# Hybrid attention/RWKV/conv block on one core: the bias masks inside the recurrence, another order of the stages, 128-row query-key passes and a token-major softmax

## The chip, the cores and the metric

The kernel runs on one core of one Trainium2 chip. Time is device microseconds of that core; lower is better. A run of the kernel before took 1196.58 us (median of three, 1184.8 to 1198.01). The profile shown here is one further execution.

## What is computed

One decoder layer on x of 512 tokens by 1024 channels, in float32, cut to the parts that matter here:

```python
h = rmsnorm(x) * (1 + sc1) + sh1
z_attn, z_rwkv, z_conv, z_gate = split(h @ w_in)
# attention: 8 heads of 64, an indexer picks min(256, s // 4) = 128 keys for each query
score = sum_h(relu(qi_h @ ki.T) * wi_h);  keep the top 128 causal keys
logits = q @ k.T / 8 + rel_bias[t5_bucket(pos_q - pos_k)]      # 32 buckets, 8 heads
o_attn = softmax(logits over the kept keys) @ v
o_rwkv = rwkv7_mix(z_rwkv)         # a recurrence over the tokens, group norm, gate
o_conv = c_b * causal_dwconv(c_c * c_x, sc_conv_w)
gates = sigmoid(z_gate)            # 3 branches of 1024 channels
merged = gates[0]*(o_attn @ w_b[0]) + gates[1]*(o_rwkv @ w_b[1]) + gates[2]*(o_conv @ w_b[2])
x = x + g1 * (merged @ w_o)
x = x + g2 * conv_glu_ffn(rmsnorm(x) * (1 + sc2) + sh2);  final rmsnorm
```

## The kernel before, in words

Every large product is done with both operands split into a high and a low part, so that a block of 128 rows takes three matmuls: lines 177, 178 and 179 in `mm_t` (weights as the stationary operand, 512 tokens moving) and lines 188 to 190 in `mm_n` (V columns, 256 wide). `weights` loads a raw block over the SP queue, ACT copies it to the high part (line 163) and POOL subtracts it for the low part (line 165). Such a triple for one 128x128 block is called a weight triple below. A column of z (`z_col`, 8 triples) ends in one of three PSUM banks named `mm`; everything else on TensorE uses a ring of five banks named `sd`.

A scheduler sets the order on each engine: it takes the program text as the order of importance and pulls work forward whose inputs and buffers are free. Weight triples of later stages thereby stand as filler between the small steps of the serial stages. `tc.high_priority` with a negative offset makes a step less important than its place says; `tc.issue_after` keeps it behind a named instruction.

The stages in the order of time: the norm, columns of z for the RWKV branch; the solve of 31 steps on DVE (lines 569 and 571), whose result goes through DRAM and back (`blk`, `Dm`) and becomes `TT`; the recurrence over 8 chunks of 64 tokens (lines 604 to 645: `Xs`, line 610, from products at 608; `UV`, line 619, from products at 617; the state `S`, lines 636 and 638, from products at 625; each has a fresh `sd` bank); group norm and the output of that branch (lines 669 to 674); the conv columns (lines 693 to 702), pulled forward by the scheduler into the solve and the recurrence; the columns of the attention (`att_cols`), with the bias masks and some `ada` steps between them; the V columns (line 188 on); the indexer (`two_pass`, lines 800 and 801, relu on ACT, weighted sum on DVE, lines 832 and 834) and the top 128 by 16 rounds of MAX8 and MATCH_REPLACE8 for each query block (lines 839 and 840); the attention; three branches with gates, `w_o`, the feed-forward part.

The bias. `posq` holds the key-side positions, `thr` 32 thresholds for each of four key blocks. For a key block b and half of the thresholds, 16 masks (`mk`, line 721, DVE, 0 or 1 in f16) of 128 by up to 512 queries are made; 32 matmuls of 128x32 with `dmat` for each query block (line 727) turn them into the bias of 8 heads; ACT scales them into `stage` (line 733, two instructions for each bank) and a DMA writes them to `bias_d` in DRAM.

The attention. For each of four head pairs and each of four query blocks, POOL adds the top-128 mask to the bias tile `bt` (line 867). `two_pass` makes the logits: the first pass has the key's high part on both halves of the 128 rows against the query's high and low part, the second the key's low part against the query's high part on 64 rows. DVE adds the bias and takes the maximum (line 874), negates it (line 876), ACT takes exp and the sum (line 878), DVE scales the probabilities (line 881), TensorE transposes them (line 885), ACT copies them to `pT` (line 889); after four query blocks, line 894 multiplies `pT` with V and ACT copies the result to `o_at` (line 897). `merged` of the branches lies in a left pool that is opened after the attention's pools are closed; the first write to it follows the gates (line 920).

`ada` are 96 pieces of the conditioning matrix, each a load and one multiply-add on DVE (line 217); they can stand anywhere before the feed-forward part and are handed out in portions, by `next(ada, None)`.

Of the kernel before, what the change touches and what calls it, by code (L numbers as in the profile page):

```python
# [20 lines left out]
H, HD = 8, 64  # L21
# [38 lines left out]
def hybrid_block(ctx, tc, ins, out, consts, dbg=None, stop=99):  # L60
# [286 lines left out]
    def rel_pos(name, shape, aps, pos0, pool, keep=None):  # L347

        pi, lo_i = (T(name + x, shape, I32, pool=pool) for x in "il")
        for dst, ap in aps:  # L350
            SP.dma_start(dst(pi), ap)
        DVE.tensor_scalar(lo_i, pi, 0xFFFF, None, op0=ALU.bitwise_and)
        DVE.tensor_scalar(pi, pi, 16, None, op0=ALU.arith_shift_right)
        rel = T(name, shape, pool=keep or pool)
# [3 lines left out]
        return rel  # L358

    def bias_operands():  # L360
# [7 lines left out]
        thr = rel_pos("thr", [128, 4, 32], [  # L368
            ((lambda t, b=b: t[:, b, :]), dram("positions", b * 128, [[0, 32], [32, 4], [1, 32]])) for b in range(4)], pos0, start.pool, sb)
        DVE.tensor_scalar(thr, thr, kc[:, K_THR:K_THR + 1], None, op0=ALU.add)  # L370
# [25 lines left out]
        return pos0, thr, pw, dmat  # L396

    with tc.issue_after(h_last):
        pos0, thr, pw, dmat = bias_operands()
# [155 lines left out]
    ep.close()  # L555

# [9 lines left out]
    for s_ in range(31):  # L566
# [4 lines left out]
        DVE.tensor_tensor(Ts[:, s_ + 1:, :w], Ts[:, s_ + 1:, :w], t_, op=ALU.add)  # L571
# [28 lines left out]

    S_ = None
    for c in range(8):
        if c:
# [80 lines left out]
    cvp = left_pool("cvp")  # L684
    o_cv = T("o_cv", [128, 4, 512], pool=cvp.pool)

# [6 lines left out]
    for m in range(4):  # L693
        ps_c = z_col(C_CONV + 512 + m * 128)
        cc = wk()
        ACT.activation(cc, ps_c, AF.Copy)
        ps_x = z_col(C_CONV + 1024 + m * 128)
        DVE.tensor_tensor(cc, cc, ps_x, op=ALU.mult)
        cy = wk()
        conv3(cy, cc, cw[:, m, :])  # L700
        ps_b = z_col(C_CONV + m * 128)
        DVE.tensor_tensor(o_cv[:, m, :], cy, ps_b, op=ALU.mult)  # L702
    tap("o_conv", o_cv)


    adp = left_pool("adp")
    bi = right_pool("bi")

    posq = rel_pos("posq", [128, S], [(lambda t: t, dram("positions", 0, [[0, 128], [1, S]]))], pos0, bi.pool)
    bias_d = tc.dram_tile([4, 128, H, 4, 128], F32, name="bias_d")  # L710

    def bias_steps():
        for b in range(4):
            n = S - 128 * b
            stage = {}
            for half in range(2):
# [6 lines left out]
                for qb in range(b, 4):  # L723
# [5 lines left out]
                    if half == 0:  # L729
                        stage[qb] = T("stage", [128, 8, 4, 2, 16], tag="stage", bufs=4, pool=bi.pool)  # L730
# [595 lines left out]
```

## Time and profile before

| | us |
|---|---|
| median of three runs | 1196.58 (1184.8 to 1198.01) |
| the profiled execution | 1197.88 |
| its span, first to last instruction | 1196.2 |
| TensorE busy | 1093.3 (91% of the span) |
| DVE busy | 763.9 (64%) |
| ACT busy | 447.3 (37%) |
| POOL busy | 363.7 (30%) |
| mean granted TensorE clock | 0.95 of full speed |

The profile gives for each engine the time in which it had an instruction under way; on TensorE instructions overlap, so that an instruction's duration is longer than the distance to the next one's start. A window view gives busy time and number of instructions of each engine in a stretch of the span, with the granted clock and what the DMA engines did. A line view groups instructions, with the idle time of the engine ahead of them and what ended it.

### The profile page before, as it was taken

To read this page: it belongs to the slowest core of one execution; us is meant where nothing else is said; L and a number is where in the kernel's file an instruction comes from. 1 tells how busy PE (TensorE), PEld (TensorE's weight loads), DVE (VectorE), ACT (ScalarE), POOL (GpSimd) and SP (SyncE) were. 2 spreads that over 40 slices of the span, in tenths; PEclk is the share of its full clock that TensorE was granted. 3 is DMA by queue.
4 is the path that set the end of the run, shared out by engine and by line. 5 is a ranking of instruction groups with operands and counts; after the bars stand their busy time and mean duration, and the time that the engine had idled before them with its cause. 6 is when DMAs were issued, how large, how long until landed. Compare 5 with 4: busy or idle time off the path is not lost.

```text
span 1196.2 us, 17528 instructions
## 1 busy us (share of the span) xinstructions
PE 1093.3 (91%) x6710; PEld 877.2 (73%) x6710; DVE 763.9 (64%) x1363; ACT 447.3 (37%) x765; POOL 363.7 (30%) x254
## 2 busy tenths in 40 slices
PE   4889899799999989998887999998899999999996
PEld 3667678577767875876655778877898888888885
DVE  5888777732587828798555454468866766762326
ACT  4243332132334322422333443446543444542213
POOL 3233233322222430565455210003443455200001
PEclk9899899899989975998899999999999999999998
DMA  9641123322336990279766343522233333462201
GB/s 324 183 107 42 39 75 91 88 61 60 115 98 193 302 247 9 76 208 233 211 186 152 91 132 101 176 84 89 75 85 106 87 90 106 141 229 92 97 5 71
DMA packets 191074, 148.26 MB, mean 124 GB/s; under 512 B 18148, under 2 KB 167038, under 8 KB 190990
## 3 DMA queue, kind: packets, MB, share of 16 engines
q1 hardware_dynamic: 162605, 122.57, 35.5%
q10 hardware_dynamic: 23056, 14.53, 4.1%
q0 software_dynamic: 5328, 10.03, 3.8%
q8 instruction: 53, 0.87, 0.3%
q14 instruction: 32, 0.25, 0.1%
HBM read 128.48 MB, written 18.63 MB: 123 GB/s over the span
## 4 chain that ended last, share of the span: by engine, by line
PE 59%; DVE 21%; issue 8%; DMA 7%; ACT 3%; POOL 2%; SPq 0%; ACTq 0%; DVEq 0%; POOLq 0%
PE mm L177 6%; PE mm L179 6%; PE mm L178 6%; DMA xraw<-in_ada_w 3%; PE sd L177 2%; PE sd L178 2%; PE sd L179 2%; PE sd L801 2%; PE sd L1250 2%; PE sd L1252 2%; PE sd L1251 2%; PE sd L1047 2%; DVE acc L217 2%; PE sd L1049 2%; PE sd L1048 2%
## 5 line engine op out<-in xcount | busy, mean ns | idle before, releaser
L165 POOL TENSOR_TENSOR wlo<-wraw,whi 128x1024 fp32r<-128x1024 f32 (+1 forms) x70 | 157.1, 2246 | 279.6 <-ACT whi L163 222.1
L178 PE MATMUL mm<-h_lo,whi 128*128 128x512 f32 (+2 forms) x496 | 203.3, 410 | 1.5 <-DVE h_lo L1076 1.5
L177 PE MATMUL mm<-h_hi,whi 128*128 128x512 f32 (+2 forms) x496 | 203.7, 412 | 0.7 <-DVE o_cv L702 0.7
L179 PE MATMUL mm<-h_hi,wlo 128*128 128x512 f32 (+2 forms) x496 | 203.4, 410 | 0.0
L163 ACT ACTIVATE whi<-wraw 128x1024 fp32r<-128x1024 f32 (+1 forms) x86 | 80.2, 935 | 221.2 <-PE mm L178 95.2
L178 PEld LDWEIGHTS mm<-h_lo,whi 128*128 128x128 f32 (+1 forms) x496 | 96.2, 194 | 24.5 <-issue 3.3
L177 PEld LDWEIGHTS mm<-h_hi,whi 128*128 128x128 f32 (+1 forms) x496 | 96.0, 194 | 23.0 <-issue 4.2
L179 PEld LDWEIGHTS mm<-h_hi,wlo 128*128 128x128 f32 (+1 forms) x496 | 96.3, 194 | 22.1 <-issue 2.4
L1017 DVE TENSOR_TENSOR wlo<-wraw,whi 128x1024 fp32r<-128x1024 f32 x46 | 64.5, 1403 | 58.9 <-ACT whi L1016 58.3
L1016 ACT ACTIVATE whi<-wraw 128x1024 fp32r<-128x1024 f32 x46 | 48.7, 1059 | 75.7 <-PE sd L1252 27.7
L217 DVE SCALAR_TENSOR_TENSOR acc<-xraw,ccol,acc 128x512 f32<-128x512 f32 x56 | 55.7, 994 | 26.1 <-DMA xraw<-in_ada_w 25.7
L1034 POOL TENSOR_TENSOR fS<-wraw 128x512 f32<-128x512 f32 x13 | 19.8, 1526 | 155.3 <-DMA wraw<-in_ffn_w_up 142.5
L1047 PE MATMUL sd<-mg_hi,shi 128*128 128x256 f32 x156 | 45.1, 289 | 7.8 <-DVE p L1190 7.8
L1017 DVE TENSOR_TENSOR slo<-wraw,shi 128x1024 fp32r<-128x1024 f32 x28 | 34.9, 1247 | 21.6 <-ACT shi L1016 21.5
L721 DVE TENSOR_SCALAR mk<-posq,thr 128x512 f16<-128x512 f32 (+3 forms) x128 | 44.7, 424 | 4.1 <-PE sd L727 4.1
L1293 POOL TENSOR_TENSOR f<-f 128x512 f32<-128x512 f32 x4 | 5.7, 1415 | 134.8 <-ACT wk L993 134.8
L177 PE MATMUL sd<-h_hi,whi 128*128 128x512 f32 x112 | 44.5, 397 | 0.0
L1048 PE MATMUL sd<-mg_lo,shi 128*128 128x256 f32 x156 | 44.4, 285 | 0.0
L1049 PE MATMUL sd<-mg_hi,slo 128*128 128x256 f32 x156 | 44.4, 285 | 0.0
L178 PE MATMUL sd<-h_lo,whi 128*128 128x512 f32 x112 | 44.3, 396 | 0.0
L179 PE MATMUL sd<-h_hi,wlo 128*128 128x512 f32 x112 | 44.2, 395 | 0.0
L177 PE MATMUL mm<-o,whi 128*128 128x512 f32 x96 | 39.9, 416 | 3.2 <-DVE modc L203 3.2
(521 smaller groups left out, 2780.7 us busy)
## 6 DMA issues: line engine op xcount, KB each, us to landing
wraw<-in_w_in SPq DMA_DIRECT2D x61, 512.0 KB, 4.3
xraw<-in_ada_w SPq DMA_DIRECT2D x96, 256.0 KB, 4.4
wraw<-in_ffn_w_up SPq DMA_DIRECT2D x44, 512.0 KB, 3.9
wraw<-in_ffn_w_down SPq DMA_DIRECT2D x22, 512.0 KB, 3.4
wraw<-in_w_branch SPq DMA_DIRECT2D x24, 256.0 KB, 3.8
bias_d<-stage ACTq DMA_DIRECT2D x10, 512.0 KB, 5.2
wraw<-in_w_o SPq DMA_DIRECT2D x8, 512.0 KB, 3.8
z_att<-wk ACTq DMA_DIRECT2D x12, 256.0 KB, 2.2
```

The source lines that it names most:

```text
L163: ACT.activation(hi, raw, AF.Copy)
L165: lo_engine[0].tensor_tensor(lo, raw, hi, op=ALU.subtract)
L177: PE.matmul(ps, hi[:, k, :], ahi[:, k0 + k, :], start=start and k == 0, stop=False)
L178: PE.matmul(ps, hi[:, k, :], alo[:, k0 + k, :], start=False, stop=False)
L179: PE.matmul(ps, lo[:, k, :], ahi[:, k0 + k, :], start=False, stop=stop and k == kt - 1)
L217: DVE.scalar_tensor_tensor(acc, raw, ck, acc, op0=ALU.mult, op1=ALU.add)
L721: DVE.tensor_scalar(m_[:, :n], posq[:, b * 128:], thr[:, b, gg:gg + 1], None, op0=ALU.is_ge)
L1016: ACT.activation(hi, src, AF.Copy)
L1017: DVE.tensor_tensor(lo, src, hi, op=ALU.subtract)
L1047: PE.matmul(ps, w[0][:, k], b[0][:, k], start=first and k == 0, stop=False, skip_group_check=True)
L1048: PE.matmul(ps, w[0][:, k], b[1][:, k], start=False, stop=False, skip_group_check=True)
L1049: PE.matmul(ps, w[1][:, k], b[0][:, k], start=False, stop=k == 3, skip_group_check=True)
```

## The change

1. The bias masks. `bias_steps` now stands ahead of the recurrence, and one step (16 masks, their matmuls, the ACT evictions and the DMAs) is offered at the head of each chunk and then ahead of each attention column, with a priority 3000 lower than its place. Query blocks are taken in pairs, so a mask is at most 256 wide: 192 masks (128 of 256, 64 of 128) in the place of 128 (32 each of 512, 384, 256, 128). The stage of a bank is one ACT instruction (20) in the place of two (40), and a half goes to DRAM at once: 20 DMAs of 256 KB in runs of 256 bytes in the place of 10 of 512 KB.
2. `thr` is worked out from `posq` after the solve; at the start, the four loads and six DVE instructions for it are gone.
3. The conv columns stand behind the attention in the text.
4. The loads of the indexer's operands (`qi`, `ki`, `wiT`) stand right behind the columns they come from, all on POOL. The pools `att` and `ix` are opened earlier, that of `ada` later; the `ada` steps between the attention columns are gone, and a gate takes three of them in the place of four.
5. `two_pass`: the low part of the key is loaded onto both halves, so the second pass takes 128 rows as the first does (and adds the product of the two low parts). `kl` needs two DMAs in the place of one.
6. The softmax: the DVE step gives the negated maximum at once; exp of a head follows its own maximum; the probabilities are not scaled (line 881 is gone, and 876). `pT` of one head and query block is the stationary operand and V moves (line 873 of the changed kernel: 80 matmuls of 128x64 in the place of 64 of up to 512 columns), the result `o_tok` is scaled by 1/sum on DVE (16 instructions), and 16 transposes bring it back to `o_at`. `o_tok` and two buffers of `kl` and `pT` make the attention's pool about 2 KB per partition larger.

```diff
+    posq = T("posq", [128, S], pool=bi.pool)
+    with tc.issue_after(sub_last):
+        rel_pos(posq, dram("positions", 0, [[0, 128], [1, S]]))
+        thr = T("thr", [128, 4, 32])
...
+    def bias_steps():
+        for b in range(4):
+            for qbs in [q for q in ((0, 1), (2, 3)) if q[1] >= b]:
+                qbs = [q for q in qbs if q >= b]
+                n = 128 * len(qbs)
+                for half in range(2):
+                    mk = []
+                    for g in range(16):
+                        gg = half * 16 + g
+                        m_ = T("mk", [128, 256], F16, tag="mk", bufs=17, pool=bi.pool)
+                        DVE.tensor_scalar(m_[:, :n], posq[:, qbs[0] * 128:qbs[0] * 128 + n], thr[:, b, gg:gg + 1], None, op0=ALU.is_ge)
+                        mk.append(m_)
+                    for i, qb in enumerate(qbs):
+                        ps = sd_bank()
...
+                        stage = T("stage", [128, 8, 64], tag="stage", bufs=2, pool=bi.pool)
+                        ACT.activation(stage, ps.rearrange("p (k h) -> p h k", h=8), AF.Copy, scale=pw[:, 0:1])
+                        ACT.dma_start(bias_d[qb, :, :, b, half * 64:half * 64 + 64], stage)
+                    yield
+    def bias_step():
+        with tc.high_priority(offset=-3000), tc.issue_after(sub_last):
+            next(bias, None)
     S_ = None
     for c in range(8):
+        bias_step()
         if c:
             px = sd_bank()
...
     def att_cols(c0, slot, scale):
         for i in range(4):
-            if slot == 1:
-                next(ada, None)
-            if slot < 2:
-                next(bias, None)
+            bias_step()
             split_out(z_att[slot, i], z_col(c0 + i * 128), scale)
...
     def two_pass(ps, q, hh, q0, k_hi, k_lo, n):
-        r = slice(hh * 64, hh * 64 + 64)
         PE.matmul(ps[:, :n], q[:, hh, q0:q0 + 128], k_hi[:, :n], start=True, stop=False)
-        PE.matmul(ps[:, :n], q[r, hh, q0:q0 + 128], k_lo[r, :n], start=False, stop=True)
+        PE.matmul(ps[:, :n], q[:, hh, q0:q0 + 128], k_lo[:, :n], start=False, stop=True)
...
-        kh, kl = M("kh", [128, 2, 512], F32R), M("kl", [128, 512], F32R)
-        for hh in range(2):
-            POOL.dma_start(kh[hh * 64:(hh + 1) * 64], z_att[1, pr, :, 0, :].rearrange("(h r) t -> r h t", h=2))
-        POOL.dma_start(kl, z_att[1, pr, :, 1, :])
-        pT = M("pT", [128, 4, 640], bufs=1)
+        kh, kl = M("kh", [128, 2, 512], F32R), M("kl", [128, 2, 512], F32R)
+        for i, k in enumerate((kh, kl)):
+            for hh in range(2):
+                POOL.dma_start(k[hh * 64:(hh + 1) * 64], z_att[1, pr, :, i, :].rearrange("(h r) t -> r h t", h=2))
+        o_tok = M("o_tok", [128, 4, 128])
...
-                DVE.tensor_tensor_reduce(lg[hh][:, :n], ps[:, :n], bt[:, hh, :n], 1.0, -3.0e38, op0=ALU.add, op1=ALU.max,
+                DVE.tensor_tensor_reduce(lg[hh][:, :n], ps[:, :n], bt[:, hh, :n], -1.0, 3.0e38, op0=ALU.add, op1=ALU.min,
                                          accum_out=rs[:, 0, hh:hh + 1])
-            DVE.tensor_scalar(rs[:, 1], rs[:, 0], -1.0, None, op0=ALU.mult)
+                ACT.activation(lg[hh][:, :n], lg[hh][:, :n], AF.Exp, bias=rs[:, 0, hh:hh + 1], scale=-1.0,
+                               accum_out=rs[:, 1, hh:hh + 1])
+            DVE.reciprocal(rs[:, 2], rs[:, 1])
+            po = sd_bank()
             for hh in range(2):
-                ACT.activation(lg[hh][:, :n], lg[hh][:, :n], AF.Exp, bias=rs[:, 1, hh:hh + 1], accum_out=rs[:, 2, hh:hh + 1])
-            DVE.reciprocal(rs[:, 0], rs[:, 2])
-            for hh in range(2):
-                DVE.tensor_scalar(lg[hh][:, :n], lg[hh][:, :n], rs[:, 0, hh:hh + 1], None, op0=ALU.mult)
...
+                pT = M("pT", [128, 512])
+                ACT.activation(pT[:, :n], pt[:, :n], AF.Copy)
+                h = 2 * pr + hh
+                for b in range(qb + 1):
+                    PE.matmul(po[:, hh * 64:(hh + 1) * 64], pT[:, b * 128:(b + 1) * 128], vtok[:, b, h * 64:(h + 1) * 64],
+                              start=(b == 0), stop=(b == qb))
+            DVE.tensor_tensor(o_tok[:, qb].rearrange("p (h d) -> p h d", h=2), po[:, :128].rearrange("p (h d) -> p h d", h=2),
+                              rs[:, 2].unsqueeze(2).to_broadcast([128, 2, 64]), op=ALU.mult)
...
+    for m in range(4):
+        ps_c = z_col(C_CONV + 512 + m * 128)
...
     branch(1, split_o(o_rw), True, False)
```

How the instructions stand on the engines. TensorE of the kernel before, from the end of chunk 0 of the recurrence (line 625) to the products of chunk 1 (line 608); `mm<-h_hi,whi` and the like are weight triples:

```order
L625 MATMUL sd<-UV,HYL 128x64 x7
L177 MATMUL mm<-h_hi,whi 128x512
L178 MATMUL mm<-h_lo,whi 128x512
L179 MATMUL mm<-h_hi,wlo 128x512
L608 MATMUL sd<-S,AR 64x64
L177 MATMUL mm<-h_hi,whi 128x512
L608 MATMUL sd<-S,AR 64x64 x7
```

One triple lies between the two steps. TensorE of the changed kernel, where chunk 0 ends (line 663 is the former 625); the triples that begin here are followed by more of their kind:

```order
L663 MATMUL sd<-UV,HYL 128x64
L177 MATMUL mm<-h_hi,whi 128x512
L178 MATMUL mm<-h_lo,whi 128x512
L179 MATMUL mm<-h_hi,wlo 128x512
L177 MATMUL mm<-h_hi,whi 128x512
L178 MATMUL mm<-h_lo,whi 128x512
L179 MATMUL mm<-h_hi,wlo 128x512
L663 MATMUL sd<-UV,HYL 128x64 x7
```

And TensorE of the changed kernel around the products of chunk 1 (line 646 is the former 608; lines 624 are the mask matmuls):

```order
L624 LDWEIGHTS mk
L624 MATMUL sd<-dmat,mk 128x32
L646 MATMUL sd<-S,AR 64x64 x8
L624 LDWEIGHTS mk
L624 MATMUL sd<-dmat,mk 128x32
```

Between the last two pieces, that is between chunk 0 and chunk 1, the changed order has 345 matmuls of lines 177 to 179, all 192 of the V columns (lines 188 to 190) and the mask matmuls of one bank after another; from chunk 1 to the end of the recurrence it has 48 matmuls of lines 177 to 179 and masks.

DVE of the kernel before, in two chunks of the recurrence:

```order
L636 TENSOR_TENSOR S<-sd,Sp 64x256 x2
L610 TENSOR_TENSOR Xs<-sd,MV 128x256
L619 COPY UV<-sd 64x4x64
L753 SCALAR_TENSOR_TENSOR wk<-mm,wk 128x512
L636 TENSOR_TENSOR S<-sd,Sp 64x256 x2
```

DVE of the changed kernel in chunk 1 (lines 648, 657, 674 are the former 610, 619, 636):

```order
L648 TENSOR_TENSOR Xs<-sd,MV 128x256
L618 TENSOR_SCALAR mk<-posq,thr 128x256 x4
L657 COPY UV<-sd 64x4x64
L618 TENSOR_SCALAR mk<-posq,thr 128x256 x7
L674 TENSOR_TENSOR S<-sd,Sp 64x256 x2
L618 TENSOR_SCALAR mk<-posq,thr 128x256 x4
L618 TENSOR_SCALAR mk<-posq,thr 128x128
L648 TENSOR_TENSOR Xs<-sd,MV 128x256
```

Between the steps of one chunk now stand 9 to 24 masks, 16 in this one. TensorE in the attention of the kernel before, where the logits of a query block are made (`qs`, `kh`, `kl`) and the probabilities of the one ahead of it are transposed (`lg`):

```order
L179 MATMUL mm<-h_hi,wlo 128x512
L885 MATMUL sd<-ident,lg 128x128 x2
L177 MATMUL mm<-h_hi,whi 128x512
L885 MATMUL sd<-ident,lg 128x128 x2
L800 MATMUL sd<-kh,qs 128x384
L801 MATMUL sd<-kl,qs 128x384
L800 MATMUL sd<-kh,qs 128x384
L801 MATMUL sd<-kl,qs 128x384
L178 MATMUL mm<-h_lo,whi 128x512
```

TensorE of the changed kernel in the attention (line 868 transposes, line 873 multiplies with V):

```order
L873 MATMUL sd<-vtok,pT 128x64 x2
L801 MATMUL sd<-kl,qs 128x384
L868 MATMUL sd<-ident,lg 128x128 x3
L873 MATMUL sd<-vtok,pT 128x64 x3
L868 MATMUL sd<-ident,lg 128x128 x3
L800 MATMUL sd<-kh,qs 128x512
L801 MATMUL sd<-kl,qs 128x512
L800 MATMUL sd<-kh,qs 128x512
L873 MATMUL sd<-vtok,pT 128x64 x3
```

No weight triple stands there. ACT of the changed kernel at the end of the attention (line 861 is the exp, 870 the copy of the transposed probabilities, 880 the copy to `o_at`, 914 the first write to `merged`):

```order
L870 ACTIVATE pT<-sd 128x384 x2
L861 ACTIVATE lg,rs<-lg,rs 128x512 x2
L870 ACTIVATE pT<-sd 128x512 x2
L880 ACTIVATE o_at<-sd 128x512
L914 ACTIVATE merged<-mm 128x512 x3
L163 ACTIVATE whi<-wraw 128x512
L914 ACTIVATE merged<-mm 128x512
```

The three `mm` banks that are emptied into `merged` are emptied behind the last step of the attention.

## Rows read from the trace of the kernel before

**Rows 1.** By stage: window, its length, busy us (instructions) per engine, clock, DMA.
```profile
190.00:230.00 40.00, 37.38 (x160) 29.45 (x158) 36.23 (x70) 7.04 (x8) 12.49 (x5) 1.00 0.30 79
255.00:310.00 55.00, 54.51 (x572) 42.35 (x572) 18.16 (x36) 15.86 (x33) 12.27 (x10) 1.00 0.18 51
346.00:402.00 56.00, 55.31 (x743) 40.59 (x743) 49.97 (x139) 22.12 (x46) 13.89 (x5) 0.94 0.65 190
...
438.00:470.00 32.00, 32.00 (x73) 17.11 (x72) 21.18 (x59) 9.24 (x20) 4.22 (x4) 0.56 0.21 67
470.00:570.00 100.00, 92.09 (x378) 71.47 (x377) 84.21 (x152) 32.22 (x50) 55.28 (x36) 0.92 0.63 162
570.00:703.00 133.00, 116.30 (x502) 81.92 (x501) 74.45 (x174) 50.57 (x125) 51.96 (x39) 0.95 0.57 148
703.00:800.00 97.00, 96.83 (x427) 78.08 (x426) 50.09 (x67) 37.48 (x55) 5.86 (x6) 1.00 0.49 142
703.00:1196.00 493.00, 466.55 (x2635) 403.11 (x2633) 291.32 (x394) 204.88 (x322) 115.13 (x81) 0.99 0.35 105
```

**Rows 2.** The same windows for line 178 alone (one per weight triple): TensorE, weight loads, clock, DMA.
```profile
190.00:703.00 513.00, 165.85 (x393) 77.17 (x392) 0.92 0.53 142
255.00:310.00 55.00, 13.46 (x31) 5.84 (x31) 1.00 0.18 51
...
570.00:703.00 133.00, 37.17 (x89) 17.48 (x88) 0.95 0.57 148
703.00:1196.00 493.00, 94.66 (x258) 48.54 (x258) 0.99 0.35 105
```

**Rows 3.** Single lines: count, duration ns min/median/max, first and last start in us.
```profile
L571 DVE TENSOR_TENSOR sub<-sub,st x31: 191/374/2598, 192.4 to 229.5; 128x31 f32<-128x31 f32 x2, 128x60 f32<-128x60 f32 x2, 128x87 f32<-128x87 f32 x2, 128x112 f32<-128x112 f32 x2
...
L617 PE MATMUL sd<-MV,TT x16: 218/218/267, 254.9 to 257.5; 64*64 64x64 f32 x16
...
L617 PE MATMUL sd<-Xs,TT x112: 218/218/267, 263.4 to 305.4; 64*64 64x64 f32 x112
...
L721 DVE TENSOR_SCALAR mk<-posq,thr x128: 270/407/2483, 345.9 to 401.6; 128x512 f16<-128x512 f32 x32, 128x384 f16<-128x384 f32 x32, 128x256 f16<-128x256 f32 x32, 128x128 f16<-128x128 f32 x32
...
L800 PE MATMUL sd<-ki,qi x24: 383/522/687, 439.1 to 497.8; 128*128 128x256 f32 x8, 128*128 128x384 f32 x8, 128*128 128x512 f32 x8
...
L840 DVE MATCH_REPLACE8 sc<-m,sc x48: 408/554/685, 452.2 to 555.5; 128x256 f32<-128x256 f32 x16, 128x384 f32<-128x384 f32 x16, 128x512 f32<-128x512 f32 x16
...
L894 PE MATMUL sd<-pT,vtok x64: 272/436/1116, 604.8 to 702.5; 128*64 128x512 f32 x16, 128*64 128x384 f32 x16, 128*64 128x256 f32 x16, 128*64 128x128 f32 x16
```

**Rows 4.** Lines of DVE from 190 to 230 us: busy us, mean ns, idle before.
```profile
L691 DVE SCALAR_TENSOR_TENSOR wk<-wk,cw 128x510 f32<-128x510 f32 x2 | 3.6, 1818 | 0.0
...
L690 DVE SCALAR_TENSOR_TENSOR wk<-wk,cw 128x511 f32<-128x511 f32 x2 | 1.5, 744 | 0.0
L698 DVE TENSOR_TENSOR wk<-wk,mm 128x512 f32<-128x512 f32 x2 | 1.4, 684 | 1.0 <-PE mm L179 1.0
L702 DVE TENSOR_TENSOR o_cv<-wk,mm 128x512 f32<-128x512 f32 x2 | 1.4, 678 | 0.0
```

**Rows 5.** Timeline of TensorE late in the attention: start us, duration, line.
```profile
692.85 0.50 PE L801 MATMUL sd<-kl,qs 64*128 64x512 f32 x1
693.28 0.50 PE L800 MATMUL sd<-kh,qs 128*128 128x512 f32 x1
...
694.47 0.39 PE L179 MATMUL mm<-h_hi,wlo 128*128 128x512 f32 x1
694.70 0.40 PE L177 MATMUL mm<-h_hi,whi 128*128 128x512 f32 x1
```

**Rows 6.** `ada` steps on DVE from 438 to 570 us.
```profile
L217 DVE SCALAR_TENSOR_TENSOR acc<-xraw,ccol,acc 128x512 f32<-128x512 f32 x26 | 27.2, 1046 | 5.3 <-DMA xraw<-in_ada_w 5.1
```

**Rows 7.** Line 881 on DVE in the window of the attention.
```profile
570.00:703.00 133.00, 16.86 (x32) 0.95 0.57 148
```

**Rows 8.** Line 876 on DVE from 570 to 703 us.
```profile
L876 DVE TENSOR_SCALAR rs<-rs 128x2 f32<-128x2 f32 x16 | 3.8, 240 | 0.3
```

More of the change, by code (lines that the diff above doesn't have):

```diff
@@ L344, in hybrid_block, with rel_pos @@
     columns("B")
[L347 to L351, printed above, removed]
+    def rel_pos(rel, src):
+        pi, lo_i = (T("wk", [128, 512], I32, tag="wk", bufs=4) for _ in range(2))
+        SP.dma_start(pi, src)
         DVE.tensor_scalar(lo_i, pi, 0xFFFF, None, op0=ALU.bitwise_and)
         DVE.tensor_scalar(pi, pi, 16, None, op0=ALU.arith_shift_right)
-        rel = T(name, shape, pool=keep or pool)
         DVE.tensor_scalar(rel, pi, pos0[:, 0:1], 65536.0, op0=ALU.subtract, op1=ALU.mult)
@@ L555, in hybrid_block @@
     ep.close()
+    bi = left_pool("bi")
     sp = right_pool("sp")
@@ L770, in hybrid_block @@
     ACT.dma_start(z_wi, t[64:72])
+    vtok = T("vtok", [128, 4, 512], pool=att.pool)
+    sel = {0: cmask}
+    for qb in range(1, 4):
+        sel[qb] = T("sc", [128, (qb + 1) * 128], tag="sc%d" % qb, pool=att.pool)
+    qi = T("qi", [128, 4, 2, 384], F32R, pool=ix.pool)
+    for i in range(4):
+        load_q(qi[:, i], z_att[2, i], 128, 384)
+    ki = T("ki", [128, 2, 512], F32R, pool=ix.pool)
+    for hh in range(2):
+        POOL.dma_start(ki[hh * 64:(hh + 1) * 64], z_ki)
+    wiT = T("wiT", [8, 512], pool=ix.pool)
+    POOL.dma_start(wiT, z_wi)
     att_cols(C_ATT, 0, HD ** -0.5)
@@ L890, in hybrid_block @@
-        po = sd_bank()
-        for b in range(4):
-            for hh in range(2):
-                h = 2 * pr + hh
-                PE.matmul(po[hh * 64:(hh + 1) * 64, b * 128:], vtok[:, b, h * 64:(h + 1) * 64],
-                          pT[:, b, (b + 1) * 128:] if hh == 0 else pT[:, 3 - b, :(4 - b) * 128],
-                          start=(b == 0), stop=(b == 3), skip_group_check=True)
+                    PE.transpose(pt[:, b * 128:(b + 1) * 128], lg[hh][:, b * 128:(b + 1) * 128], ident)
+                pT = M("pT", [128, 512])
@@ L897, in hybrid_block @@
+        po = sd_bank()
+        for qb in range(4):
+            PE.transpose(po[:, qb * 128:(qb + 1) * 128], o_tok[:, qb], ident)
         ACT.activation(o_at[:, pr, :], po, AF.Copy)
@@ L945, in split_o @@
         return o
+    for m in range(4):
+        ps_c = z_col(C_CONV + 512 + m * 128)
+        cc = wk()
+        ACT.activation(cc, ps_c, AF.Copy)
+        ps_x = z_col(C_CONV + 1024 + m * 128)
+        DVE.tensor_tensor(cc, cc, ps_x, op=ALU.mult)
+        cy = wk()
+        conv3(cy, cc, cw[:, m, :])
+        ps_b = z_col(C_CONV + m * 128)
+        DVE.tensor_tensor(o_cv[:, m, :], cy, ps_b, op=ALU.mult)
+    tap("o_conv", o_cv)
     branch(1, split_o(o_rw), True, False)
```

106 lines of the change are left out of this document (27 added, 79 removed).

## The prediction

> **What bounds the kernel now.** I read the stages first [rows 1]: windows laid between the first and last starts of single lines [rows 3]. The columns are the length of a stretch, each engine's busy time, and the clock. TensorE is busy nearly everywhere, but with two kinds of work. From 703 us to the end it is dense: 467 of 493 us busy, full clock. Before that the stages are serial chains (solve on DVE, recurrence, top 128 on DVE, softmax), and TensorE is full there because weight triples of later stages fill the gaps. How many, a view of line 178 alone tells [rows 2]: 393 triples from 190 to 703 us, of these 89 in the attention, against 258 after it. So the question is not what TensorE's work costs, but which triples still find a gap. Every triple that finds none lands in the dense part at full price. That price comes from the timeline [rows 5]: start to start 694.47 to 694.70, 0.23 us for one matmul of 512 columns.
>
> **The change part by part.** I count matmuls of lines 177 to 179 in the two orders. From the start to the last step of the attention the kernel before has 1433, the changed one 948. Of the 485 that are missing none is gone: behind the attention there are 775 before and 1260 now. They cost 485 x 0.233 = 113 us in the dense part. What is bought for it is an earlier end of the attention, now at 703 us (the last start of line 894, 702.5, [rows 3]). So the change pays only if the attention ends before 703 - 113 = 590 us. I follow the chain to that point.
>
> The solve. It runs from 192.4 to 229.5 [rows 3]; the conv's DVE steps in it take 3.6 + 1.5 + 1.4 + 1.4 = 7.9 us [rows 4] and stand behind it now; a little waiting goes too: -9 us, so it ends at about 220. The way through DRAM is unchanged, and chunk 0, whose first products start at 254.9 [rows 3], starts at about 246.
>
> Chunk 0 to chunk 1. Before, one triple stands between them. Now 345 matmuls of triples and 192 of the V columns do, because the products of chunk 1 need one of five `sd` banks, and the banks ahead of it in the ring go to bias steps that stand far down in the order. TensorE does things in order, so the chain waits for all of them: 345 x 0.233 + 192 x 0.117 (half as wide, half the price) = 103 us. This is the largest single term. It isn't lost, since those triples are done, but it is done in front of the recurrence, not in its gaps. Chunk 0 (7 us) at 246, chunk 1 at 356.
>
> Chunks 1 to 7. Before, 55 us hold all eight, with 31 triples inside [rows 1, 2], about 6.9 us each. Without the triples the chain itself bounds: I keep 7 x 6.9 = 48. Between the steps now stand about 110 masks, at 0.27 (the shortest) to 0.41 us (the median of all widths, [rows 3]) 30 to 45 us, against 55 - 18 = 37 us in which DVE was idle in all eight chunks [rows 1]. If all fit, they cost nothing; if none fits, 45. They do not lie as the gaps do (9 to 24 in a chunk), so I take about a quarter, 12. End at 416.
>
> To the indexer. Group norm and the output part took from 310 to 337 or so; I keep 27: 443. Then come the masks that are left and 120 triple matmuls, 28 us, with the masks beside them: 471. The indexer began at 439.1 [rows 3], so this is 32 us later, although the mask stage of 56 us [rows 1] is gone: what was filler there is now done ahead of chunk 1.
>
> Indexer and top 128, 439.1 to 556 [rows 3], 117 us, bound by DVE with 53 triples in its gaps or so. Of 26 `ada` steps at 1.05 us [rows 6] 14 are left: -13. Less TensorE work ahead of the relus: -6. That gives 98, so 569.
>
> The attention. 133 us hold 16 query blocks and 89 triples [rows 1, 2]; 89 x 3 x 0.233 = 62 are the triples, 71 the rest, 4.4 us a block. The scalings (16.9, [rows 7]) and the negations (3.8, [rows 8]) leave the chain: 21 / 16 = 1.3, so 3.1 us a block, 50 in all, at the least. Against this stand the transposes of the result, V as the moving operand with 80 small matmuls, six DMA issues on POOL for five, and nothing that fills. The other end is the 4.4 plus 0.9 for half the clock on the small matmuls: 5.3, 85. I take 4.1 us, 66 in all, nearer to the row. The attention ends at 635, 68 us sooner than before.
>
> No triple fills it: `merged` now lies over memory of the attention's pool, so the first write to it waits for that pool, the three `mm` banks stay full, and TensorE has nothing but the small matmuls. A forecast that counts the shorter softmax as a gain reads the wrong column: that gain is in the 68 already.
>
> The 128-row second pass. Pass to pass takes 0.43 us [rows 5], a 512-wide triple matmul 0.23; at that price two passes cost 0.47 in the place of 0.84, 0.37 us for each of 56 pairs, 21 us of TensorE at the widest. The Trainium skill (TensorEngine Tiling (Array Packing), Key Properties) says that changing the tiling mode drains the engine; the trace agrees, 0.43 against 0.23. By the rule alone the sum would be 21 us less; it is not, since in these stages TensorE now waits, so I take nothing beyond the 6 above, and 0 to 15 as the bound.
>
> The start: four loads and six DVE steps go; the mask operands are later ready anyway, and weight triples set the pace there: 0, with 3 us as the bound.
>
> Sum: 635 + 113 + 493 = 1241, and 1.7 us outside the span; that execution was 1.3 above the median. Forecast: 1241 us.
>
> **The rivals.**
> *Faster.* The freed solve, masks that fit into the recurrence for nothing (-12), the attention at 3.1 us a block (-16), top 128 with no competition (-15) and a chain of chunks without triples at 5.5 us (-10): attention's end at 582, 1188. With the stretch before the indexer shorter by another 12, 1176. For it: DVE stands idle 37 of 55 us in the recurrence [rows 1]. Against: every term has to go well, since 590 is the break-even.
> *No change.* Gains and leftover balance, end of the attention at 580 to 602: 1186 to 1208.
> *Slower still, by the clock.* Where TensorE starves, its clock falls: from 438 to 470 us it was granted 0.56 of full speed, near the lower of its two levels (1.2 of 2.4 GHz), did 73 matmuls in 32 us and was busy all the time [rows 1]; dense stretches do 427 in 97. Chunks 1 to 7, the norm and the attention now have no filler. If all three fall to the lower level, TensorE's part of a chunk (54.5 us busy less 93 x 0.233 of triples, over eight chunks: 4 us, [rows 1, 2]) doubles, 7 x 4 = 28, the attention takes 85 (+19), the indexer gives nothing back (+6): 1294. The decision falls where TensorE's share of a chain exceeds the slack. The Trainium skill (TensorE: Matmul & The Clock Gate, The HAM clock gate) says that the gate halves the clock when the array has been idle; the trace agrees where clock and starvation meet. For it: the row. Against: 190 to 230 kept 1.00.
> *The masks stretch.* A mask took up to 2.48 us where the median is 0.41 [rows 3]. One such mask ahead of the steps of each chunk, 2 us x 3 steps x 7, is 42 at the worst: 1271 with the 12 taken off. The Trainium skill (SBUF — State Buffer, SBUF: two separate sides) says that VectorE and GpSimd exclude each other on a shared port pair; the trace has such long masks, among POOL's work, and shows no cause.
> *The change doesn't do what it says.* Masks in the recurrence hide only if the chain doesn't wait for them. In the order it does, and the conv columns are pulled ahead of the indexer in spite of their place in the text. That is in the sum.
>
> **How the numbers follow.** Forecast and its neighbourhood (1209 to 1265): 0.56. Slower still (clock or stretched masks): 0.14. No change: 0.13. Faster: 0.17. Range 1193 to 1272: it leaves out one in ten at each end. A difference of 1% is about what a measurement of this kernel can tell from none: faster 0.17, same 0.13, slower 0.70.
>
> **What would show it.** Right: TensorE dense for about 100 us between chunk 0 and chunk 1; no line 177 to 179 in the attention; the first write to `merged` behind the last copy to `o_at`; 485 matmuls more of lines 177 to 179 behind the attention's end; that end at 620 to 650. Wrong if the attention ends before 600, if the stretch ahead of chunk 1 is under 80 us, or if the part behind the attention is much under 600 us, by fillers that I have counted as lost or by a tail that was not TensorE-bound.

## The result

| | before | after |
|---|---|---|
| median us | 1197.3 (4 runs, 1184.8 to 1201.0) | 1295.1 (4 runs, 1291.8 to 1297.9) |
| ratio | | 1.0835, 95% interval 1.0752 to 1.0919 |
| span of the profiled execution, us | 1196.2 | 1293.7 |
| mean granted TensorE clock | 0.95 | 0.894 |

The change makes the kernel 8% slower. The direction was forecast; the size was not: 1241 was predicted, and 1295 lies beyond the range of 1193 to 1272. The experiments ran on chips on which the kernel before took 1185, 1193 and 1196 us (medians), so two runs from different chips are compared by their ratios to the kernel before, in percentage points of it.

The windows of the changed kernel, laid between the same events as [rows 1] (window, its length, busy us and instructions of TensorE, its weight loads, DVE, ACT and POOL, clock, DMA share, GB/s):

```profile
188.00:215.00 27.00, 7.21 (x31) 5.44 (x30) 24.87 (x64) 2.23 (x3) 3.82 (x2) 0.72 0.22 58
...
248.00:354.00 106.00, 105.28 (x553) 89.01 (x551) 13.98 (x16) 28.12 (x36) 43.80 (x19) 1.00 0.48 136
354.00:432.00 78.00, 66.31 (x891) 58.60 (x890) 51.53 (x149) 20.82 (x39) 11.54 (x8) 0.67 0.27 63
455.00:500.00 45.00, 42.73 (x314) 35.07 (x311) 23.11 (x66) 16.06 (x27) 11.82 (x9) 0.89 0.50 128
500.00:580.00 80.00, 30.95 (x112) 21.92 (x110) 72.21 (x181) 15.86 (x26) 16.66 (x15) 0.71 0.43 108
580.00:671.00 91.00, 69.78 (x316) 57.41 (x316) 22.81 (x98) 35.36 (x100) 35.62 (x35) 0.65 0.50 112
671.00:1293.70 622.70, 592.87 (x3184) 506.92 (x3184) 369.19 (x478) 240.78 (x377) 170.51 (x110) 0.98 0.39 118
```

The first line is the solve, where TensorE now has 31 matmuls (160 in a window of 40 us, [rows 1]). The second is new: 106 us of dense work at full clock between chunk 0 and chunk 1. Of the next four lines, the chunks, the top 128 (500 to 580) and the attention lost fillers, and the clock column tells it: 0.67 in chunks 1 to 7, where it was 1.00, 0.71 in the top 128, where it was 0.92, and 0.65 in the attention, where it was 0.95. The last is the tail, 623 us in the place of 493.

The same windows for line 178 alone, one per weight triple, answer to [rows 2]:

```profile
248.00:354.00 106.00, 45.61 (x116) 21.56 (x115) 1.00 0.48 136
354.00:432.00 78.00, 6.40 (x16) 3.01 (x16) 0.67 0.27 63
500.00:580.00 80.00, 12.28 (x28) 5.80 (x28) 0.71 0.43 108
580.00:671.00 91.00, 0.00 (x0) 0.00 (x0) 0.65 0.50 112
671.00:1293.70 622.70, 160.38 (x420) 80.50 (x420) 0.98 0.39 118
```

There is no triple in the attention, and 420 stand behind it (258 before). Single lines (count, duration ns min/median/max, first and last start), as in [rows 3]: the products of the state in chunks 1 to 7, before (line 608) and changed (646), the last copies to `o_at`, and the first write to `merged`:

```profile
L608 PE MATMUL sd<-S,AR x112: 218/218/267, 261.2 to 303.9; 64*64 64x64 f32 x112
...
L646 PE MATMUL sd<-S,AR x112: 218/311/367, 354.8 to 420.8; 64*64 64x64 f32 x112
...
L880 ACT ACTIVATE o_at<-sd x4: 597/597/597, 604.1 to 670.8; 128x512 f32<-128x512 f32 x4
...
L914 ACT ACTIVATE merged<-mm x8: 578/582/616, 671.3 to 713.1; 128x512 f32<-128x512 f32 x8
```

The products' median duration is 311 ns; it was 218. From their first and last starts a chunk takes (420.8 - 354.8) / 6 = 11.0 us; it was 7.1. The write to `merged` starts at 671.3, right behind the last copy to `o_at` at 670.8.

### The profile page after: what moved, and what is told of

Read it like the earlier page. It is cut to its first block, busy times and chain, and to the rows that moved or that the text cites. A ratio compares the mean times of both kernels' runs of the same rounds, so it can differ in the third digit from the quotient of the medians.

```text
span 1293.7 us, 17738 instructions
## 1 busy us (share of the span) xinstructions
PE 1111.8 (86%) x6822; PEld 928.1 (72%) x6822; DVE 747.5 (58%) x1394; ACT 446.8 (35%) x746; POOL 366.9 (28%) x259
## 5 line engine op out<-in xcount | busy, mean ns | idle before, releaser
L177 PE MATMUL mm<-h_hi,whi 128*128 128x512 f32 (+2 forms) x496 | 197.9, 400 | 22.6 <-DVE wk L743 20.8
L178 PE MATMUL mm<-h_lo,whi 128*128 128x512 f32 (+2 forms) x496 | 196.2, 396 | 1.1 <-DVE h_lo L1071 1.1
L179 PE MATMUL mm<-h_hi,wlo 128*128 128x512 f32 (+2 forms) x496 | 195.9, 395 | 1.2 <-POOL wlo L165 1.2
L217 DVE SCALAR_TENSOR_TENSOR acc<-xraw,ccol,acc 128x512 f32<-128x512 f32 x56 | 58.9, 1051 | 21.1 <-DMA xraw<-in_ada_w 20.3
L618 DVE TENSOR_SCALAR mk<-posq,thr 128x256 f16<-128x256 f32 (+1 forms) x192 | 58.6, 372 | 11.4 <-PE sd L624 11.2
L873 PEld LDWEIGHTS sd<-vtok,pT 128*128 128x128 f32 x160 | 31.7, 280 | 18.5 <-ACT pT L870 17.4
```

The costliest lines, as they stand in the source:

```text
L177: PE.matmul(ps, hi[:, k, :], ahi[:, k0 + k, :], start=start and k == 0, stop=False)
L178: PE.matmul(ps, hi[:, k, :], alo[:, k0 + k, :], start=False, stop=False)
L179: PE.matmul(ps, lo[:, k, :], ahi[:, k0 + k, :], start=False, stop=stop and k == kt - 1)
L217: DVE.scalar_tensor_tensor(acc, raw, ck, acc, op0=ALU.mult, op1=ALU.add)
L618: DVE.tensor_scalar(m_[:, :n], posq[:, qbs[0] * 128:qbs[0] * 128 + n], thr[:, b, gg:gg + 1], None, op0=ALU.is_ge)
```

## The experiments

Three theories stood after the result. Theory A: the order decides; triples that find no gap in a serial stage are paid in full elsewhere, and a few couplings (shared memory, shared rings, priority) took the gaps away. Theory B: fillers lengthen the chain in which they stand by what they save the tail, so that moving them changes nothing. Theory C: the rewritten parts themselves (masks, softmax, V product) are slower. The clock is a part of A that had to be measured by itself.

### Two kilobytes nobody uses (b_pad2k)

```diff
     M = lambda name, shape, dt=F32, bufs=2: T(name, shape, dt, bufs=bufs, pool=sm.pool)
+    pad = M("pad", [128, 512], bufs=1)
     for pr in range(4):
```

> The kernel before, with one tile of 2 KB per partition added to the attention's pool that nothing reads or writes. Theory A (the missing triples): the pool now reaches 512 bytes into the memory of merged, the first write to merged waits for the attention's end, and the order loses 485 matmuls of triples from the top-128 and the attention: 1260 of them behind the attention in the place of 775. 485 x 0.233 = 113 us more behind it, an attention that ends at 630 to 650 in the place of 703: 1240 to 1270 us. Theory B (fillers cost the chain what they save the tail): the attention gets shorter by the 113 us that it no longer holds, and the time stays at 1185 to 1210. Theory C (the rewritten softmax and the masks are what costs): nothing of them is in this kernel, so 1185 to 1210.

Measured: 1245.3 us (1242.1 to 1247.7), ratio 1.0496 (1.045 to 1.0542). The windows of its attention and of its tail, and the attention for line 178 alone:

```profile
515.00:631.00 116.00, 66.94 (x211) 39.84 (x212) 37.01 (x132) 36.08 (x101) 32.91 (x31) 0.58 0.35 81
631.00:1245.90 614.90, 586.51 (x3175) 500.20 (x3173) 367.49 (x469) 241.13 (x377) 167.66 (x111) 0.99 0.39 116
...
515.00:631.00 116.00, 0.00 (x0) 0.00 (x0) 0.58 0.35 81
```

The first writes to `merged`, in the kernel before (line 931) and here (932):

```profile
L931 ACT ACTIVATE merged<-mm x8: 578/582/595, 485.4 to 547.4; 128x512 f32<-128x512 f32 x8
...
L932 ACT ACTIVATE merged<-mm x8: 578/582/617, 631.3 to 670.5; 128x512 f32<-128x512 f32 x8
```

This is what theory A said. The computation is the one of before; only addresses moved, by enough to put the attention's pool 512 bytes into the memory of `merged` (153504 to 169888 per partition; the pool begins at 169376 with this tile). The first write to `merged` now stands behind the attention's last step. The attention ends 72 us sooner (631 against 703), the tail is 121 longer, for 485 more matmuls of triples. Theory B falls, since moving triples changed the time. Theory C can't explain this kernel, in which nothing was rewritten; whether it adds something in the changed one is left to b_two and b_soft. One more thing is in these rows: without its 89 triples the old attention takes 116 us in the place of 133. The fillers' 62 us of TensorE had cost the stage 17.

### The changed kernel without that overlap (a_otok1)

```diff
-        o_tok = M("o_tok", [128, 4, 128])
+        o_tok = M("o_tok", [128, 4, 128], bufs=1)
```

> The changed kernel with one buffer of o_tok in the place of two; the attention's pool then ends below merged. In the order 311 matmuls of triples come back ahead of the attention's end (949 behind it in the place of 1260). Theory A: the tail gets 311 x 0.233 = 72 us shorter, the top-128 and the attention together 10 to 30 longer, TensorE's clock in the attention near 1.0 in the place of 0.65: 1235 to 1260 us. Theory B: what leaves the tail comes back in the attention, 1280 to 1300.

Measured: 1243.0 us (1237.5 to 1249.2), ratio to before 1.0489 (1.0422 to 1.0557), 3.5 percentage points less than the changed kernel (1.0835). Recurrence, attention and tail:

```profile
355.00:430.00 75.00, 62.82 (x877) 55.29 (x873) 51.05 (x149) 20.25 (x39) 11.52 (x8) 0.72 0.28 64
581.00:698.00 117.00, 97.06 (x520) 78.31 (x520) 55.35 (x132) 50.29 (x123) 62.57 (x52) 0.90 0.83 188
698.00:1238.20 540.20, 511.74 (x2845) 440.53 (x2844) 326.18 (x439) 215.12 (x338) 123.37 (x83) 0.98 0.37 113
```

The attention is 26 us longer, the tail 82 shorter. The recurrence is nearly as it was, 75 us at 0.72 of the clock.

### The bias steps at the priority of their place (a_prio0)

```diff
-        with tc.high_priority(offset=-3000), tc.issue_after(sub_last):
+        with tc.issue_after(sub_last):
             next(bias, None)
```

> The changed kernel with the bias steps at the priority of their place (without the offset of -3000). In the order the 346 matmuls of triples and 192 of the V columns between chunk 0 and chunk 1 are gone from there and stand later, 161 of the triples in the attention, 163 ahead of it beside the top-128; behind the attention there are 1260 as in the changed kernel. Theory A1 (work in front of the recurrence is time, work in gaps is not): chunk 1 starts at about 252 in the place of 355, the attention ends at 590 to 625 in the place of 671, 1215 to 1250 us in all. Theory B1 (the same matmuls ahead of the same tail, so the same time): 1280 to 1300.

Measured: 1206.7 us (1202.0 to 1210.3), ratio to before 1.017 (1.012 to 1.022), 6.7 points less than the changed kernel. The time is a little under what was expected, on a chip where the kernel before took 1185 us. Products of the state, recurrence, attention and tail:

```profile
L646 PE MATMUL sd<-S,AR x112: 217/219/268, 252.5 to 306.6; 64*64 64x64 f32 x112
...
252.00:316.00 64.00, 59.69 (x859) 49.09 (x858) 48.08 (x136) 23.08 (x44) 12.19 (x10) 0.97 0.39 101
471.00:582.00 111.00, 96.69 (x519) 77.41 (x517) 28.84 (x103) 57.37 (x125) 61.74 (x52) 0.94 0.69 147
582.00:1200.20 618.20, 591.71 (x3184) 506.60 (x3184) 367.27 (x478) 240.47 (x376) 169.15 (x110) 0.98 0.39 119
```

The tail still has all 1260 matmuls. What fell away is that the same work stood in front of the recurrence, where DVE was busy for 14 of 106 us, while in the top 128 TensorE was busy for 31 of 80 us and the attention had no triple. The products are back at 219 ns, and a chunk takes (306.6 - 252.5) / 6 = 9.0 us with the masks, against 11.0 in the changed kernel and 7.1 before.

### A bank of their own for the bias matmuls (a_bias_bank)

```diff
-        return pp.tile([128, 512], F32, name="sd", tag="sd", bufs=5)
+        return pp.tile([128, 512], F32, name="sd", tag="sd", bufs=4)
+    def bias_bank():
+        return pp.tile([128, 512], F32, name="bb", tag="bb", bufs=1)
...
-                        ps = sd_bank()
+                        ps = bias_bank()
```

> The changed kernel with one of the five sd banks kept for the bias matmuls alone (four for the rest), still 3000 lower in priority. If it is the shared ring of banks that makes chunk 1 wait for the triples, chunk 1 starts at 248 to 258 us in the place of 355, in spite of the low priority; the masks then come late, 574 of 640 mask matmuls in the attention, which waits for them: 1230 to 1300 in all. If the priority alone is the reason, chunk 1 stays at about 355.

Measured: 1250.6 us (two runs, 1248.5 and 1252.7), ratio to before 1.0476 (1.0374 to 1.0578). The products of the state:

```profile
L649 PE MATMUL sd<-S,AR x112: 218/218/267, 255.2 to 298.5; 64*64 64x64 f32 x112
```

Chunk 1 starts at 255.2 with the low priority unchanged, and a_prio0 starts it at 252.5 with the shared ring unchanged. So neither held it back alone: a low priority did so by way of a ring that it shared with urgent steps. The masks, now free to be late, are late: the last one starts at 528.7, when the first logits have long been made (455.0). The attention pays; its last copy to `o_at` is at 624.9, where a_prio0 has it at 581.3.

### Keeping TensorE at work in the attention (a_warm)

```diff
             po = sd_bank()
+            for _ in range(6):
+                PE.matmul(po, q[:, 0, qb * 128:qb * 128 + 128], kh[:, 0], start=True, stop=True)
             for hh in range(2):
```

> The changed kernel with six extra matmuls of 128x512 for each query block of the attention, into the bank that the V product overwrites; they do nothing but keep TensorE at work while the softmax runs (16 x 6 x 0.233 = 22 us at full clock, 45 at half). If the attention's 91 us in the changed kernel come from TensorE's clock (0.65 granted there), the clock rises to 0.85 or more, and the attention takes 76 to 88 us with the added work, 1278 to 1293 us in all. If the clock is beside the point, the extra matmuls only stand in the way: 95 to 115 us, 1298 to 1320.

Measured: 1273.7 us (1269.0 to 1276.2), ratio to before 1.0714 (1.0659 to 1.0769): with 96 matmuls added, the changed kernel is 1.2 points faster, some 14 us. The attention, and in it the added matmuls and the V product:

```profile
582.00:657.00 75.00, 68.31 (x406) 56.79 (x406) 22.86 (x98) 35.23 (x100) 35.70 (x35) 0.93 0.62 136
```

```profile
L866 PE MATMUL sd<-kh,qs 128*128 128x512 f32 x90 | 25.0, 416 | 0.0
L875 PE MATMUL sd<-vtok,pT 128*128 128x64 f32 x160 | 22.5, 285 | 0.5 <-ACT pT L872 0.4
```

The clock goes from 0.65 to 0.93 and the attention from 91 to 75 us, with the same work on DVE, ACT and POOL. The V product's mean is 285 ns. In the changed kernel, in the window of 582 to 657, it is

```profile
L873 PE MATMUL sd<-vtok,pT 128*128 128x64 f32 x132 | 29.0, 373 | 9.0 <-ACT pT L870 8.9
```

so the clock was worth 16 us of this stage, the time of the added matmuls included, by a kernel that differs in nothing else. The Trainium skill (TensorE: Matmul & The Clock Gate, Why this matters for your kernels) advises to leave no idle gaps between bursts of matmuls; this pair of runs agrees with it, 0.65 with the gaps and 0.93 with them filled by work that is thrown away.

### The 128-row second pass alone (b_two)

The kernel before with the low keys on both halves (`kl` of [128, 2, 512], two DMAs) and the second pass on 128 rows, as in part 5 of the change:

```diff
-        PE.matmul(ps[:, :n], q[r, hh, q0:q0 + 128], k_lo[r, :n], start=False, stop=True)
+        PE.matmul(ps[:, :n], q[:, hh, q0:q0 + 128], k_lo[:, :n], start=False, stop=True)
```

> The kernel before with the 128-row second pass and the doubled low keys alone. Its pool reaches into merged as that of b_pad2k does and the order has the same 1260 matmuls of triples behind the attention, so b_pad2k (1245 us) is what it is to be compared with. If a change of the row tiling costs TensorE time in the chain of a block, 16 blocks and 24 pairs of the indexer give 8 to 20 us back: 1225 to 1238. If TensorE's passes stand beside the waits of the softmax, or the sixth DMA issue on POOL takes the gain, 1240 to 1255.

Measured: 1235.2 us (1232.5 to 1236.5), ratio to before 1.0392 (1.0342 to 1.0443), against 1.0496 for b_pad2k with the same number of triples behind the attention. About 1% is the gain of the passes (the intervals just miss each other); in the attention it is 9 us:

```profile
515.00:622.00 107.00, 55.00 (x211) 38.46 (x210) 37.63 (x130) 36.67 (x102) 34.48 (x34) 0.61 0.43 95
```

### The softmax and V product alone (b_soft)

The kernel before with part 6 of the change, and its keys as they were.

> The kernel before with the rewritten softmax and token-major V product alone. Up to the attention nothing changes (first logits at about 564). In the order 154 matmuls of triples stand in the attention in the place of 278, 899 behind it in the place of 775 (+29 us). If the rewrite shortens the chain as the prediction had it (3.1 to 4.1 us a block without triples), the attention takes 36 + 50 to 66 = 86 to 102 us and the total is 1185 to 1200; if the small matmuls with 128x128 weight loads make a block 5.7 us, as the changed kernel's attention has it, 127 us and 1215 to 1230.

Measured: 1194.3 us (1187.4 to 1205.3), ratio 1.0053 (1.0015 to 1.0092): no gain. The logits' first passes start at 557.8 and the last copy to `o_at` at 660.3; in the kernel before at 564.5 and 702.8. The shorter attention (-42 us at its end) is given back by 124 triple matmuls that now stand behind it: that part takes 529 us in the place of 493.

That the rewrite is slower (theory C) is not so. With no triple in either, and the 128-row passes in both, the attention takes 107 us with the old softmax (b_two) and 91 with the new one (the changed kernel). What is left of theory C are the masks in the recurrence, 1.9 us a chunk in a_prio0.

### Both, with the pool kept out of merged (b_soft_two_otok1)

> The kernel before with the rewritten softmax, the 128-row second pass and one buffer of o_tok, so that the attention's pool ends below merged; masks, conv and ada as before. In the order 167 matmuls of triples stand in the attention (154 in b_soft) and 886 behind it (899). If both parts of the attention's rewrite are gains once the memory of merged is left alone: b_soft (1194) less 3 for the triples and 5 to 15 for the passes, 1176 to 1188. If the two-sided keys bring nothing: 1188 to 1196.

Measured: 1179.7 us (1173.5 to 1184.3), ratio 0.9915 (0.9877 to 0.9953): the attention's part of the change is a small gain, 0.9%, once it leaves `merged` alone.

### The bias steps early, without the overlap (ao_p1000)

`offset=1000` in the place of -3000, and `o_tok` with one buffer.

> The changed kernel with one buffer of o_tok and the bias steps at a priority 1000 higher than their place, in the place of 3000 lower. In the order there are 21 matmuls of triples between chunk 0 and chunk 1, 128 in the seven chunks behind, 421 beside the second half of the top-128 and in the attention, and 1163 behind the attention in the place of 1260 (a_prio0). Theory A (triples in gaps are free): the attention ends at 580 to 600 as in a_prio0 and the tail of 619 us gets 97 x 0.25 = 24 us shorter: 1175 to 1195 us, below the kernel before or level with it. Theory B (each filler lengthens the chain that it stands in): 1200 to 1215.

Measured: 1181.5 us (1172.1 to 1191.6, 12 runs), ratio 0.995 (0.9911 to 0.999), as theory A had it: the last copy to `o_at` starts at 578.0, and the whole is about level with the kernel before.

### rel_pos with tiles of another ring (a_st, ao_p1000_st)

In the solve of the changed kernel, the waits of TensorE's loads, TensorE and ACT name one chain (engine, line, releaser, us in total, times, longest):

```profile
PEld mm L177 <- DVE wk L743: 21.2, 1, 21.2
PE mm L177 <- DVE wk L743: 20.8, 1, 20.8
ACT wk L742 <- DVE wk L354: 20.3, 1, 20.3
```

`wk` is a ring of four work tiles. A column of the attention can't be emptied by ACT (line 742) until `rel_pos` (line 354) has let go of a `wk` tile; two of the four are its own, and it runs after the solve.

```diff
-        pi, lo_i = (T("wk", [128, 512], I32, tag="wk", bufs=4) for _ in range(2))
+        pi, lo_i = (T("stage", [128, 512], I32, tag="stage", bufs=2, pool=bi.pool) for _ in range(2))
```

> The changed kernel (1295 us) with the two tiles of rel_pos from the ring of stage, nothing else. In the order 96 matmuls of triples go from the stretch between chunk 0 and chunk 1 into the solve (433 ahead of chunk 0 in the place of 337). Theory A3: that stretch of 103 us gets 96 x 0.233 = 22 us shorter and everything behind it comes 18 to 25 us sooner, 1270 to 1280. Rival (the solve, filled, takes longer by as much): 1290 to 1300.

Measured for the changed kernel with this line alone: 1280.8 us (1277.5 to 1285.8), ratio to before 1.072 (1.0636 to 1.0804), 1.2 points less than the changed kernel. The intervals of the two overlap, but the trace shows where it comes from: chunk 1 starts at 339.9 in the place of 354.8. That is a little short of what was expected; the solve, with the columns' steps on DVE in it, ends at 224 in the place of 214.

> ao_p1000 (1181.5 us) with the two tiles of rel_pos taken from the ring of stage in the place of the ring of wk. Theory A3: rel_pos holds two of the four wk tiles until the solve is over, so that the columns of the attention can't be emptied in the solve and TensorE starves there; with its own tiles 435 matmuls of triples stand ahead of chunk 0 in the place of 339, 1090 behind the attention in the place of 1163. The solve's gap of 200 to 250 us is filled at full clock, the tail 73 x 0.25 = 18 us shorter, the chain the same or a little longer: 1155 to 1170. Rival: the solve is bound by DVE, what is put into it comes out of the recurrence's gaps, 1175 to 1190.

Measured: 1175.0 us (1168.5 to 1181.2), ratio 0.9838 (0.9778 to 0.9897). The solve and the recurrence:

```profile
188.00:215.00 27.00, 27.00 (x117) 20.62 (x117) 20.99 (x39) 8.32 (x12) 11.54 (x5) 1.00 0.60 181
215.00:255.00 40.00, 32.62 (x410) 25.58 (x409) 35.20 (x78) 12.59 (x18) 11.24 (x5) 0.80 0.53 142
255.00:320.00 65.00, 65.00 (x824) 54.33 (x825) 37.45 (x126) 20.52 (x37) 13.17 (x10) 0.91 0.45 119
```

TensorE has 117 matmuls in the stretch of the solve where it had 31, at full clock. But the time is above the 1155 to 1170 that were expected and at the edge of the rival's range. What is behind the attention got 19 us shorter than in ao_p1000 (591 to 572), as expected; but the solve ends at 228.0 where ao_p1000 has it at 213.4, and the last copy to `o_at` starts at 603.0 where it has it at 578.0. In these two traces the filled solve lengthens the chain by as much as it takes from the tail, which is what the rival said. With the memory, the priority and this ring put right, the change is 1.6% faster than the kernel before; on these runs it has the lowest ratio. Its interval lies just below that of ao_p1000 (0.9911 to 0.999), on another chip, but the profiled execution of ao_p1000 was the shorter one (span 1170.0 against 1175.8), and it overlaps that of b_soft_two_otok1 (0.9877 to 0.9953). That it is faster than either is not shown beyond doubt.

### The masks behind the recurrence again (best_norec)

ao_p1000_st without `bias_step()` at the head of a chunk.

> ao_p1000_st without the bias steps ahead of the chunks: all twelve stand ahead of the attention columns, behind the recurrence, as in the kernel before. Tells what the masks in the recurrence are worth once nothing else is in the way. If the recurrence hides them: its period goes from about 9 to 7.1 us a chunk without them (-13), and the stretch between the recurrence and the indexer gets longer by 448 mask matmuls and 125 masks of DVE, 40 to 50 us: 20 to 35 us slower than ao_p1000_st. If the recurrence gives back what it hides: within 10 us of it.

Measured: 1193.0 us (1180.7 to 1198.9, 12 runs), ratio 0.9985 (0.9942 to 1.0028), on the same chip 18 us more than ao_p1000_st. A chunk goes from (329.9 - 268.7) / 6 = 10.2 to (305.8 - 261.1) / 6 = 7.5 us, and still the whole is slower: hiding the masks in the recurrence is worth 1.5%, a little less than expected.

## Why the prediction was right and wrong

**Right: the mechanism of the largest term, and what the order does.** The first products of chunk 1 were put at 356 us and came at 354.8; the 345 triple matmuls and the V columns took 103 us by the sum and the window of 106 us holds them. No triple in the attention, `merged` behind it, 485 matmuls moved: as stated. The solve was thought to end at 220 and ended at 214. From there the profiled execution gathers 53 us: -1 at the start of chunk 1, +17 in the chunks, +4 up to the indexer, -9 in the indexer and the top 128, +25 in the attention, +17 in the tail.

**Wrong: the attention, 66 us. The step that failed is "62 are the triples, 71 the rest, 4.4 us a block".** It takes the fillers' TensorE time out of a stage as if the rest stayed as it is. The attention took 91 us, outside the bound of 85. b_pad2k has the old attention without a triple, and that is 116 us and not 71: the triples had stood in time in which TensorE otherwise waited, and without them the clock was 0.58 in the place of 0.95. The changes themselves gave more than the 5 us that were counted for them: 9 by the 128-row passes (116 to 107), which were put at nothing here, and 16 by the softmax (107 to 91), 1.0 us a block where 1.3 was the most. a_warm puts the clock's part in the changed kernel at 16 us or more; how the 45 us between 71 and 116 divide into clock and overlap was not measured.

**Wrong: the chunks, 48 + 12 us, by the same step.** "Without the triples the chain itself bounds: I keep 7 x 6.9 = 48." The changed kernel takes 11.0 us a chunk, 77 in seven. The 12 for the masks were right in size: a_prio0 has nearly as many masks there (103 against 117) at a clock of 0.97 and takes 9.0, 1.9 over the kernel before, 13 in seven. The other 2.0, 14 in all, are put down to the clock: products of 311 ns and not 218, at 0.67. That part is argued from this pair of runs, which differ in the triples between the steps too; no run raised the clock of the chunks alone.

**Too small: the tail, 113 + 493 = 606 us.** It took 623. TensorE was busy for 126 us more there than before [rows 1], so it is the one that got longer. The count left out 64 small matmuls of the `ada` steps, which came along with the triples:

```profile
L202 PE MATMUL mm<-one,acc x64: 164/250/271, 492.7 to 677.0; 128*128 128x1 f32 x64
...
L202 PE MATMUL mm<-one,acc x64: 164/250/250, 683.0 to 829.1; 128*128 128x1 f32 x64
```

In the kernel before (first line) they end ahead of the tail, in the changed one they stand in it, for 7.6 us of TensorE. With as many triples behind the attention the tail is 615 in b_pad2k, 616 in a_warm and 618 in a_prio0; the up to 8 us between these kernels were not looked into.

**Mixed: the way to the indexer, and the indexer.** From the last output matmul (453.7) to the first score (491.1) it took 37 us, where 28 were put. The indexer and the top 128 then took 89 where 98 were put, so that they ended at 580 and not at 569. The count of "53 triples" in them was a wrong reading: the kernel before has 108 from 439 to 556 us, the changed one 28 from 491 to 580.

**The range.** The clock rival was worked out as 1294 us and came within a microsecond. That is partly luck, since its terms miss in both directions: it had +28 in the chunks (14 by the account above), +19 in the attention (25), +6 in the indexer (-9), and nothing for the tail (17). Its direction was right: it alone let starved stages run at a lower clock. It was given one in seven together with the stretched masks. The row that spoke against it, "190 to 230 kept 1.00", was of a stage full of conv triples; in the changed kernel, without them, that very stage fell to 0.72. A stage's clock was read as a property of the stage, when it is one of what fills it.

**Not so: the stretched masks.** The longest mask took 2.57 us, but the median is 341 ns over 192 masks, and the 117 of them in the chunks took 37.0 us, 316 ns each.

**What the size of the change was made of.** In the kernel before, the overlap alone costs 5.0%; taken out of the changed kernel it gives 3.5 points, the priority 6.7, the ring of `wk` 1.2. They add up to more than the 8.35 that were lost: each decides where the others' triples may go. With all three put right, what is left of the change is worth 1.6%. Its other parts (thresholds after the solve, the conv behind the attention, the moved loads and `ada` steps) were not run alone.

## What to carry to other kernels

In a kernel whose serial stages are filled with later matmuls, ask of each change which fillers it still lets in: a pool that grows by 2 KB, two tiles borrowed from a ring or a low priority in a shared ring of banks can each cost about as much as the change saves, or more. Count the filler matmuls per stage in the order before and after. Do not price a stage that loses them as its old time less the fillers' (71 us here, where 116 were measured), and allow for a lower clock: the starved stages here were granted 0.58 to 0.72. Something that has a lower priority must not take from a ring that something urgent waits for.

## What was not expected of the hardware

Ninety-six matmuls whose results are thrown away made a stage that waits for ACT and DVE most of the time 16 us faster (91 to 75), with the granted clock at 0.93 instead of 0.65. And 512 bytes of overlap between the attention's pool and a tile of a later stage made the kernel before 5.0% slower, with not one instruction of the computation changed.
